# Stick-breaking attention: the reverse scan over the keys in pieces of 512 columns, right piece first

## The chip, the core and the metric

The kernel runs on one core of one Trainium2 chip. What counts is the device time of one execution in microseconds (us). Of the kernel before, three runs took 2499.8, 2501.02 and 2506.05 us; the median is 2501.02 us. The core has four engines that compute, each with its own queue of instructions in fixed order: TensorE (PE in the profile, with its weight loads listed apart as PEld), VectorE (DVE), ScalarE (ACT) and GpSimd (POOL). SyncE (SP) issues the transfers.

## What is computed

One layer of a hybrid decoder block on 1024 tokens of width 1024: a mixing sub-layer (stick-breaking attention with 16 heads of width 64, a state-space mixer and two gates), cross-attention into 256 memory tokens, and a dense SwiGLU layer. The change lies in the stick-breaking attention (the short description of the change calls it cross attention and speaks of maxima; the lines that it edits are those of this attention, and the scan is a running product with a floor). Cut to what matters:

```python
for blk in range(seq // SB_BLOCK):              # 8 blocks of 128 queries
    t0, t1 = blk * SB_BLOCK, (blk + 1) * SB_BLOCK
    z = jnp.einsum('bhtd,bhsd->bhts', qf[:, :, t0:t1], kf[:, :, :t1])
    causal = jnp.arange(t1)[None, :] < (t0 + jnp.arange(SB_BLOCK))[:, None]
    log_1mb = jnp.where(causal, jax.nn.log_sigmoid(-z), 0.0)
    tail = lax.cumsum(log_1mb, axis=3, reverse=True)
    w = jnp.where(causal, jnp.exp(z + tail), 0.0)
    outs.append(jnp.einsum('bhts,bhsd->bhtd', w, vf[:, :, :t1]))
```

With n = sigmoid(-z), the sum of logarithms becomes a running product of n from the right end of a row of keys to its left end. The weight of a key is the difference of two neighbouring products, and the kernel moves that difference over to the values, which it holds ready as differences of neighbouring rows (`dv_d`).

## The kernel before

**A head.** The 1024 queries of a head are eight blocks (b = 0 to 7) of 128. Block b sees the first (b + 1) x 128 keys. Blocks 0 to 3 are half 0, blocks 4 to 7 are half 1. `scores` works on one block: for each piece of up to 512 keys it issues two matmuls (L935, L936, tile `sc`; the second adds the low parts of the keys, `kl`) and a sigmoid on ScalarE (L937) into the tile `n`. When the whole row is there, one VectorE instruction (L939) runs over it from right to left in place: state = max(state x n, mask), from 1.0. The mask is 1 on and right of the diagonal and 0 elsewhere, so that the state stays 1 until the first visible key and is then the product. Block 4 thus has one scan of 640 columns, block 5 of 768, block 6 of 896 and block 7 of 1024.

**The values.** `values` works on one half. Step i takes the 128 keys of chunk i: `tr(i)` transposes those columns of each of the half's blocks on TensorE into one PSUM bank (L953, tile `tr`, two banks in turn); ScalarE takes 1 off and rounds to the high part (L956, `wth`); VectorE makes the low part (L957, `wtl`), which frees the bank. `av(i - 3)`, three steps behind, multiplies both parts with the values (L965, L966, tile `av`, one bank); ScalarE empties that bank at the end of a half (L969, `oT`). Chunk 0 comes first, and chunk 0 is the left end of each row, which the scan writes last.

**What surrounds them.** Each half's values are interleaved with the scores of the next half and with the q and k projections of a later pair of heads (L126 to L128, tile `mm`), as filler on TensorE. The projection's results go through ScalarE and VectorE (L891 to L902, tile `gt`) and then by transfer into `kh`, `kl` and `qs` (L884). VectorE also splits the projection's weights (L123, `wlo`).

**What sets the order.** The code gives every engine its work in the order of these interleaved lists, and a scheduler that goes by a simulated timeline then moves instructions of an engine past each other where no dependency forbids it. One tie is written by hand: the scan of block 6 (the seventh) is issued behind `lows[h, 0, 2]`, which is the `wtl` of chunk 2 in half 0 of the same head.

Of the kernel before, what the change touches and what calls it, by code (L numbers as in the profile page):

```python
# [12 lines left out]
ALU = mybir.AluOpType  # L13
# [4 lines left out]
S = 1024  # L18
# [3 lines left out]
HALF = 512  # L22
# [32 lines left out]
def hybrid_block(ctx, tc, a, out, dbg=None):  # L55
    nc = tc.nc
    V, A, T = [InTurn(tc, e) for e in (nc.vector, nc.scalar, nc.tensor)]
# [12 lines left out]
    def mk(pl, shape, dt, tag, bufs=None):  # L70
        uid[0] += 1
        kw = {} if bufs is None else {"bufs": bufs}
        return pl.tile(shape, dt, tag=tag, name=f"{tag}_{uid[0]}", **kw)
# [144 lines left out]
    def behind(marks):  # L218

        st = ExitStack()  # L220
        for m in marks:
            st.enter_context(tc.issue_after(m.ins))
        return st
# [52 lines left out]
    with ExitStack() as pa:  # L276
# [548 lines left out]
        with ExitStack() as p2:  # L825
# [13 lines left out]
            mask = mk(cb_, [P, S], BF16, "mask")  # L839
# [3 lines left out]
            marks, sig, highs, lows = [], [], [], {}  # L843
# [74 lines left out]
            def values_of(h):  # L918

                vt = heads[h]["v"] = mk(vp, [P, NCH, P], F32R, "v")  # L920
                nc.sync.dma_start(vt.bitcast(F32).rearrange("p c d -> p (c d)"), dv_d[h])

            def scores(h, half, tb, ns_):
                def run():
                    hd = heads[h]
                    if half == 0 and tb == 0:
                        values_of(h)
                    b = half * 4 + tb
                    L = (b + 1) * P
                    nt = mk(bp, [P, (half + 1) * HALF], F32, f"n{half}")  # L930
                    ns_.append(nt)
                    for s0 in range(0, L, HALF):
                        s1 = min(L, s0 + HALF)
                        ps = mk(psc, [P, HALF], F32, "sc")[:, :s1 - s0]
                        T.matmul(ps, hd["qs"][:, b * P:(b + 1) * P], hd["kh"][:, s0:s1], start=True, stop=False)  # L935
                        marks.append(T.matmul(ps, hd["qs"][:, b * P:(b + 1) * P], hd["kl"][:, s0:s1], start=False, stop=True))  # L936
                        sig.append(A.activation(nt[:, s0:s1], ps, AF.Sigmoid, scale=-(HD ** -0.5)))  # L937
                    with behind([lows[h, 0, 2]] if b == 6 else []):
                        V.tensor_tensor_scan(nt[:, 0:L][:, ::-1], nt[:, 0:L][:, ::-1], mask[:, S - L:][:, ::-1], 1.0, ALU.mult, ALU.max)  # L939
                return run  # L940

            LAG = 3
# [64 lines left out]
            for m in range(NM):  # L1007
                h, half = m // 2, m % 2
                hp, r = m // 4, m % 4
                s1 = [scores((m + 1) // 2, (m + 1) % 2, tb, ns_[m + 1]) for tb in range(4)] if m + 1 < NM else []  # L1010
# [1285 lines left out]
```

## Time and profile before

| what | before |
|---|---|
| median of three runs | 2501.02 us |
| the profiled execution, its own time | 2500.25 us |
| its span | 2498.5 us |
| TensorE busy over the span | 2438.4 us (98%) |
| VectorE, ScalarE, GpSimd busy | 1807.4 (72%), 1167.0 (47%), 604.5 us (24%) |
| L939, the scans: 128 of them | 170.0 us on VectorE |
| attention, 690 to 1000 us: TensorE, VectorE, ScalarE busy | 302.21, 233.66, 188.01 of 310 us |

The attention takes the stretch from about 660 to 1080 us of the span. One pair of heads repeats every 49.4 to 49.7 us in it. In a row of the timeline, the numbers are start and duration in us, then engine, line, operation, tile written and tile read, shape and count, and in brackets the idle time ahead of it on its engine with what ended it. Rows that belong together are merged ("x2"). Matmuls overlap: one of 512 columns lasts 0.39 us in the rows, and the next starts 0.23 us after it.

### The profile page before, as it was taken

To read this page: it belongs to the slowest core of one execution; us is meant where nothing else is said; L and a number is where in the kernel's file an instruction comes from. 1 tells how busy PE (TensorE), PEld (TensorE's weight loads), DVE (VectorE), ACT (ScalarE), POOL (GpSimd) and SP (SyncE) were. 2 spreads that over 40 slices of the span, in tenths; PEclk is the share of its full clock that TensorE was granted. 3 is DMA by queue.
4 is the path that set the end of the run, shared out by engine and by line. 5 is a ranking of instruction groups with operands and counts; after the bars stand their busy time and mean duration, and the time that the engine had idled before them with its cause. 6 is when DMAs were issued, how large, how long until landed. Compare 5 with 4: busy or idle time off the path is not lost. (4 is left out here: it accounts for less than half of the span.)

```text
span 2498.5 us, 33391 instructions
## 1 busy us (share of the span) xinstructions
PE 2438.4 (98%) x12306; PEld 2010.1 (80%) x12306; DVE 1807.4 (72%) x2261; ACT 1167.0 (47%) x2072; POOL 604.5 (24%) x505
## 2 busy tenths in 40 slices
PE   7999999999999999989999999999999999999998
PEld 5888788888788888877777778888888888888887
DVE  7767877767577777689888774577468556566997
ACT  5344455555465665566644312344335333344433
POOL 3221645443000000134444141102012322220001
PEclk9999999999999999999999999999999999999999
DMA  7565443333444334366332481321242322334322
GB/s 250 180 219 184 156 147 102 110 101 93 131 110 110 102 103 109 103 193 206 115 97 78 138 278 62 126 96 51 93 143 68 101 76 79 98 94 170 125 102 101
DMA packets 253741, 312.40 MB, mean 125 GB/s; under 512 B 17535, under 2 KB 169608, under 8 KB 253450
## 3 DMA queue, kind: packets, MB, share of 16 engines
q1 hardware_dynamic: 253290, 309.22, 38.8%
q8 instruction: 97, 1.59, 0.3%
q10 hardware_dynamic: 288, 1.05, 0.1%
q14 instruction: 66, 0.54, 0.1%
HBM read 210.59 MB, written 82.84 MB: 117 GB/s over the span
## 5 line engine op out<-in xcount | busy, mean ns | idle before, releaser
L939 DVE TENSOR_TENSOR_SCAN n<-n,mask 128x128 f32<-128x128 f32 (+7 forms) x128 | 170.0, 1350 | 27.7 <-ACT n L937 24.4
L123 DVE TENSOR_TENSOR sw<-sf,sw 128x512 fp32r<-128x512 f32 x142 | 127.0, 898 | 71.4 <-ACT sw L120 69.3
L120 ACT ACTIVATE sw<-sf 128x512 fp32r<-128x512 f32 x142 | 88.9, 628 | 157.4 <-PE mm L231 140.2
L956 ACT ACTIVATE wth<-tr,mone 128x512 fp32r<-128x512 f32 x192 | 110.7, 585 | 100.5 <-PE tr L953 100.1
L957 DVE SCALAR_TENSOR_TENSOR wtl<-tr,wth 128x512 fp32r<-128x512 f32 x192 | 101.8, 546 | 58.4 <-ACT wth L956 58.3
L732 DVE SCALAR_TENSOR_TENSOR b<-b,prmT,b 128x1023 f32<-128x1023 f32 (+2 forms) x72 | 110.5, 1534 | 16.9 <-ACT b L726 16.3
L123 DVE TENSOR_TENSOR sw<-wr,sw 128x512 fp32r<-128x512 f32 x107 | 98.8, 924 | 26.2 <-ACT sw L120 25.9
L230 PE MATMUL mm<-h,sw 128*128 128x512 f32 x288 | 112.0, 389 | 0.0
L231 PE MATMUL mm<-h,sw 128*128 128x512 f32 x288 | 111.7, 389 | 0.0
L116 POOL TENSOR_SCALAR whi<-wraw 128x1024 fp32r<-128x1024 f32 x13 | 14.8, 1136 | 395.0 <-PE mm L127 366.9
L229 PE MATMUL mm<-h,sw 128*128 128x512 f32 x288 | 109.9, 389 | 0.0
L197 POOL TENSOR_TENSOR sf<-wr,wr 128x512 f32<-128x512 f32 x36 | 53.1, 1476 | 228.8 <-DMA wr<-in_w_gu_dram 78.5
L126 PE MATMUL mm<-oth,bw 128*128 128x512 f32 x256 | 104.2, 407 | 4.2 <-DVE a L1289 2.6
L937 ACT ACTIVATE n<-sc 128x512 f32<-128x512 f32 (+1 forms) x192 | 86.7, 495 | 37.0 <-PE tr L953 20.6
L953 PE MATMUL tr<-ident,n 128*128 128x128 f32 x576 | 97.1, 275 | 6.1 <-DVE n L939 4.4
L128 PE MATMUL mm<-oth,bw 128*128 128x512 f32 x256 | 100.7, 393 | 0.0
L127 PE MATMUL mm<-otl,bw 128*128 128x512 f32 x256 | 100.6, 393 | 0.0
L128 PE MATMUL p<-bw,h 128*128 128x512 f32 x256 | 100.1, 392 | 0.5 <-DVE h L123 0.5
L174 POOL TENSOR_SCALAR rstd<-ms 128x1 f32<-128x1 f32 x74 | 28.0, 378 | 298.0 <-ACT x L181 226.8
L127 PE MATMUL p<-bw,h 128*128 128x512 f32 x256 | 99.9, 390 | 0.0
L126 PE MATMUL p<-bw,h 128*128 128x512 f32 x256 | 99.7, 390 | 0.0
L120 ACT ACTIVATE sw<-wr 128x512 fp32r<-128x512 f32 x107 | 67.1, 628 | 58.3 <-PE mm L231 51.4
(664 smaller groups left out, 7699.9 us busy)
## 6 DMA issues: line engine op xcount, KB each, us to landing
wr<-in_w_in_dram SPq DMA_DIRECT2D x36, 512.0 KB
wr<-in_w_gu_dram SPq DMA_DIRECT2D x72, 256.0 KB
zr<-in_w_in_dram SPq DMA_DIRECT2D x28, 512.0 KB
wraw<-in_w_in_dram SPq DMA_DIRECT2D x20, 512.0 KB
gu_d<-t SPq DMA_DIRECT2D x36, 256.0 KB
zs_d<-zo SPq DMA_DIRECT2D x32, 256.0 KB
dv_d<-v SPq DMA_DIRECT2D x16, 512.0 KB
xs_d<-b SPq DMA_DIRECT2D x32, 256.0 KB
```

The costliest lines, as they stand in the source:

```text
L120: A.activation(o, i, AF.Copy)
L123: return eng.tensor_tensor(o, i, hi.bitcast(F32), ALU.subtract)
L126: first = T.matmul(ps, sh, mh, start=start, stop=False)
L127: T.matmul(ps, sh, ml, start=False, stop=False)
L128: T.matmul(ps, sl, mh, start=False, stop=stop)
L229: T.matmul(ps, w[0][:, k, :], bh, start=first and k == 0, stop=False, skip_group_check=True)
L230: T.matmul(ps, w[0][:, k, :], bl, start=False, stop=False, skip_group_check=True)
L231: ins = T.matmul(ps, w[1][:, k, :], bh, start=False, stop=last and k == 3, skip_group_check=True)
L732: V.scalar_tensor_tensor(acc[:, sh:], y[:, :S - sh], cw(3 - sh, f), acc[:, sh:], ALU.mult, ALU.add)
L939: V.tensor_tensor_scan(nt[:, 0:L][:, ::-1], nt[:, 0:L][:, ::-1], mask[:, S - L:][:, ::-1], 1.0, ALU.mult, ALU.max)
L956: highs.append(A.activation(wh[:, t0 * P:], pt[:, t0 * P:], AF.Identity, bias=mone))
L957: lows[h, half, i] = V.scalar_tensor_tensor(wl[:, t0 * P:], pt[:, t0 * P:], -1.0, wh[:, t0 * P:].bitcast(F32), ALU.add, ALU.subtract)
```

## The change

The loop over the pieces of a row runs from right to left, so the matmuls and the sigmoid of the right piece come first. The scan moves into the loop: each piece of up to 512 columns is scanned by an instruction of its own as soon as its sigmoid is done. The right piece starts from 1.0, the left piece from the column at its right edge, nt[:, s1], which the scan ahead of it has written. Blocks 0 to 3 have one piece and are as before. Each of the blocks 4 to 7 has a right piece of 128, 256, 384 or 512 columns and a left piece of 512. Both pieces of block 6 keep the tie.

```diff
-                    for s0 in range(0, L, HALF):
+                    for s0 in range((L - 1) // HALF * HALF, -1, -HALF):
                         s1 = min(L, s0 + HALF)
                         ps = mk(psc, [P, HALF], F32, "sc")[:, :s1 - s0]
...
-                    with behind([lows[h, 0, 2]] if b == 6 else []):
-                        V.tensor_tensor_scan(nt[:, 0:L][:, ::-1], nt[:, 0:L][:, ::-1], mask[:, S - L:][:, ::-1], 1.0, ALU.mult, ALU.max)
+                        part = nt[:, s0:s1][:, ::-1]
+                        with behind([lows[h, 0, 2]] if b == 6 else []):
+                            V.tensor_tensor_scan(part, part, mask[:, S - L + s0:S - L + s1][:, ::-1], 1.0 if s1 == L else nt[:, s1:s1 + 1], ALU.mult, ALU.max)
```

The instructions are the same but for 64 more scans. Their order changes on TensorE, VectorE and ScalarE inside the attention, and at one place on SP, near its end, where three issues change places; after the attention nothing moves. The line numbers from L940 on are one higher in the changed kernel. The scan carries the name SCALAR_TENSOR_TENSOR in the listings of the order.

Place 1, VectorE, in the fifth head (in its timeline at 777.67 us). `n_1235` is the row of block 6, `n_1280` that of block 3 of the next head, `wtl_6815` (now `wtl_6835`) the low part of chunk 0 of half 1. Before:

```order
L957 SCALAR_TENSOR_TENSOR wtl_6740<-tr_6736,wth_6739 128x256
L939 SCALAR_TENSOR_TENSOR n_1235_6746<-n_1235_6746,mask_5385 128x896
L957 SCALAR_TENSOR_TENSOR wtl_6759<-tr_6756,wth_6758 128x128
L939 SCALAR_TENSOR_TENSOR n_1280_6914<-n_1280_6914,mask_5385 128x512
L957 SCALAR_TENSOR_TENSOR wtl_6815<-tr_6809,wth_6814 128x512
```

The same place in the changed kernel:

```order
L958 SCALAR_TENSOR_TENSOR wtl_6758<-tr_6754,wth_6757 128x256
L940 SCALAR_TENSOR_TENSOR n_1235_6764<-n_1235_6764,mask_5385 128x384
L958 SCALAR_TENSOR_TENSOR wtl_6778<-tr_6775,wth_6777 128x128
L940 SCALAR_TENSOR_TENSOR n_1280_6934<-n_1280_6934,mask_5385 128x512
L940 SCALAR_TENSOR_TENSOR n_1235_6764<-n_1235_6764,mask_5385 128x512
L958 SCALAR_TENSOR_TENSOR wtl_6835<-tr_6829,wth_6834 128x512
```

Block 6's left piece now stands behind `wtl` of chunk 3 and behind the scan of the next head's block 3, both of which stood behind block 6 before.

Place 2, TensorE, in the same head (timeline at 780.77 us), just after six matmuls L126 to L128. `tr_6809` (now `tr_6829`) is the bank of chunk 0 of half 1, `tr_6830` (now `tr_6850`) that of chunk 1; `n_1223`, `n_1229`, `n_1235`, `n_1242` are blocks 4, 5, 6 and 7. Blocks 4 and 5 of chunk 0 are transposed ahead of the six matmuls in both kernels. Before:

```order
L953 MATMUL tr_6809<-ident_89,n_1235_6746 128x128
L953 MATMUL tr_6809<-ident_89,n_1242_6771 128x128
L966 MATMUL av_6762<-wtl_6759,v_6552 128x128
L953 MATMUL tr_6830<-ident_89,n_1223_6702 128x128
L953 MATMUL tr_6830<-ident_89,n_1229_6723 128x128
L953 MATMUL tr_6830<-ident_89,n_1235_6746 128x128
L953 MATMUL tr_6830<-ident_89,n_1242_6771 128x128
L965 MATMUL av_6869<-wth_6814,v_6552 128x512
L953 MATMUL tr_6842<-ident_89,n_1223_6702 128x128
```

In the changed kernel:

```order
L967 MATMUL av_6781<-wtl_6778,v_6568 128x128
L954 MATMUL tr_6850<-ident_89,n_1223_6718 128x128
L954 MATMUL tr_6850<-ident_89,n_1229_6740 128x128
L954 MATMUL tr_6829<-ident_89,n_1235_6764 128x128
L954 MATMUL tr_6829<-ident_89,n_1242_6790 128x128
L954 MATMUL tr_6850<-ident_89,n_1235_6764 128x128
L954 MATMUL tr_6850<-ident_89,n_1242_6790 128x128
L966 MATMUL av_6889<-wth_6834,v_6568 128x512
L954 MATMUL tr_6862<-ident_89,n_1223_6718 128x128
```

The transposes of blocks 6 and 7 for chunk 0 moved behind half of chunk 1's, and everything of chunks 0 and 1 now ends directly ahead of the first `av` of the half. On ScalarE, `oT` of the half before moved ahead of chunk 0's `wth` there.

Place 3, TensorE, in the sixth head (timeline at 803.35 us). `n_1307` is block 6, `n_1314` block 7; `sc` with `kh` and `kl` are the scores of blocks 4 and 5 of the next half. Before, from the transposes of blocks 6 and 7 for chunk 0:

```order
L953 MATMUL tr_7079<-ident_89,n_1307_7015 128x128
L953 MATMUL tr_7079<-ident_89,n_1314_7040 128x128
L966 MATMUL av_7034<-wtl_7031,v_6822 128x128
L953 MATMUL tr_7102<-ident_89,n_1295_6974 128x128
L953 MATMUL tr_7102<-ident_89,n_1301_6995 128x128
L953 MATMUL tr_7102<-ident_89,n_1307_7015 128x128
L953 MATMUL tr_7102<-ident_89,n_1314_7040 128x128
L126 MATMUL mm_7111<-b21h_118,whi_7090 128x512
```

After that come five more matmuls of the projection, four of scores, and the first `av` of the half. In the changed kernel the six matmuls L126 to L128 and six of scores stand ahead of the transposes of blocks 6 and 7:

```order
L935 MATMUL sc_7269<-kh_6961,qs_6691 128x128
L935 MATMUL sc_7274<-kh_6961,qs_6691 128x512
L936 MATMUL sc_7274<-kl_6963,qs_6691 128x512
L935 MATMUL sc_7291<-kh_6961,qs_6691 128x256
L936 MATMUL sc_7269<-kl_6963,qs_6691 128x128
L936 MATMUL sc_7291<-kl_6963,qs_6691 128x256
L954 MATMUL tr_7103<-ident_89,n_1307_7037 128x128
L954 MATMUL tr_7103<-ident_89,n_1314_7063 128x128
L954 MATMUL tr_7126<-ident_89,n_1307_7037 128x128
L954 MATMUL tr_7126<-ident_89,n_1314_7063 128x128
L966 MATMUL av_7166<-wth_7108,v_6842 128x512
```

Further up at places 2 and 3, one pair of score matmuls of 512 columns has moved: at place 2 that of block 5's left piece, from ahead of the place to behind it, with 256 columns of its right piece taking its turn; at place 3 that of block 4's left piece, from some 1.5 us ahead of the place into the six of the list above.

## Prediction

> **What bounds the kernel now.** I read the page first, then the attention alone, since only its order moves, then what TensorE waits for in it, then the timelines of one even and one odd head.
>
> The page's span and the busy time of the engines over it:
>
> ```profile
> span 2498.5 us, 33391 instructions
> PE 2438.4 (98%) x12306; PEld 2010.1 (80%) x12306; DVE 1807.4 (72%) x2261; ACT 1167.0 (47%) x2072; POOL 604.5 (24%) x505
> ```
>
> The stretches of time, here 690 to 1010 us (length, then busy us of PE, PEld, DVE, ACT, POOL, then the granted clock):
>
> ```profile
> 690.00:1010.00 320.00, 311.65 (x1707) 260.34 (x1707) 241.63 (x297) 192.91 (x391) 7.36 (x7) 1.00 0.40 109
> ```
>
> TensorE is busy in 311.65 of 320 us at full clock, VectorE in 241.63. So TensorE bounds the attention, and VectorE matters only where TensorE stands still for it. The waits of the weight loads, which come just ahead of their matmuls, say where, over the same stretch:
>
> ```profile
> PEld tr L953 <- DVE n L939: 6.9, 7, 1.0
> PEld av L965 <- ACT oT L969: 5.9, 6, 1.0
> ...
> PEld av L966 <- DVE wtl L957: 1.3, 7, 0.2
> ...
> PEld sc L936 <- issue: 0.5, 1, 0.5
> ```
>
> Seven odd heads lose 0.98 us each to a scan, six even heads 0.98 us each to `oT`. Both lie where chunk 0 of half 1 begins. That is where the order moves, so what is asked is how long TensorE stands there afterwards.
>
> **The work added.** Groups of the scans by shape on VectorE (total, mean ns of one):
>
> ```profile
> L939 DVE TENSOR_TENSOR_SCAN n<-n,mask 128x896 f32<-128x896 f32 x16 | 32.2, 2013 | 0.0
> L939 DVE TENSOR_TENSOR_SCAN n<-n,mask 128x640 f32<-128x640 f32 x16 | 23.8, 1490 | 5.5 <-ACT n L937 2.2 <-PE av L965 2.0
> L939 DVE TENSOR_TENSOR_SCAN n<-n,mask 128x512 f32<-128x512 f32 x16 | 19.4, 1211 | 1.4 <-ACT n L937 1.4
> L939 DVE TENSOR_TENSOR_SCAN n<-n,mask 128x384 f32<-128x384 f32 x16 | 14.9, 932 | 0.0
> L939 DVE TENSOR_TENSOR_SCAN n<-n,mask 128x128 f32<-128x128 f32 x16 | 6.4, 400 | 1.4 <-ACT n L937 1.4
> ```
>
> Block 6 becomes 0.932 + 1.211 = 2.143 for 2.013 us, +0.13; block 4 0.400 + 1.211 for 1.490, +0.12. With 0.13 for each of the 64 divided rows it is 8.3 us of VectorE. The Trainium skill, "Perfetto Trace Analysis", section "Optimizing Scalar/DVE Operations", puts some 60 ns of access overhead on each VectorE instruction on SBUF, by which 64 more would be 3.8 us, less than half of what the rows give. Either sum lies on an engine that is idle for 78 of these 320 us. I cost it at nothing except in block 6, where TensorE waits for the row. Were this cover gone, the whole 8.3 us would be paid. The sigmoids and score matmuls are the same in number, and cost nothing by count.
>
> The left piece reads a column that the right one writes, so VectorE waits for itself. No row shows such a pair of scans. The nearest rows are those of VectorE below, where independent neighbours start 0.07 to 0.08 us before the one ahead ends (779.91 + 0.26 = 780.17 against 780.10; 777.98 + 2.01 = 779.99 against 779.91). A pair in order loses at least nothing and at most that and as much again, some 0.15 us; a gain has no mechanism. In block 6 another instruction stands between the pieces, so I take the overlap alone, 0.05 to 0.08, as lost there, and nothing in the others, whose first reader comes later.
>
> **An even head (the fifth).** VectorE's timeline, before:
>
> ```profile
> 774.48 1.23 DVE L123 TENSOR_TENSOR wlo<-wraw,whi 128x1024 fp32r<-128x1024 f32 x1 [0.65 <-ACT whi L120]
> ...
> 776.22 1.53 DVE L939 TENSOR_TENSOR_SCAN n<-n,mask 128x256 f32<-128x256 f32 x2
> ...
> 777.98 2.01 DVE L939 TENSOR_TENSOR_SCAN n<-n,mask 128x896 f32<-128x896 f32 x1
> 779.91 0.26 DVE L957 SCALAR_TENSOR_TENSOR wtl<-tr,wth 128x128 fp32r<-128x128 f32 x1
> 780.10 1.21 DVE L939 TENSOR_TENSOR_SCAN n<-n,mask 128x512 f32<-128x512 f32 x1
> 781.91 0.69 DVE L957 SCALAR_TENSOR_TENSOR wtl<-tr,wth 128x512 fp32r<-128x512 f32 x1 [0.60 <-ACT wth L956]
> ```
>
> From 774.48 to 781.31 VectorE has no idle time, so its order alone decides when block 6 is ready: at 779.99. TensorE and ScalarE there:
>
> ```profile
> 780.77 0.38 PE L953 MATMUL tr<-ident,n 128*128 128x128 f32 x2
> 780.91 0.31 PE L966 MATMUL av<-wtl,v 128*128 128x128 f32 x1
> 781.05 0.62 PE L953 MATMUL tr<-ident,n 128*128 128x128 f32 x4
> 782.42 0.50 PE L965 MATMUL av<-wth,v 128*128 128x512 f32 x1 [0.74 <-ACT oT L969]
> 782.75 0.60 PE L953 MATMUL tr<-ident,n 128*128 128x128 f32 x4
> 781.19 0.69 ACT L956 ACTIVATE wth<-tr,mone 128x512 fp32r<-128x512 f32 x1 [3.75 <-PE tr L953]
> ```
>
> Block 6 was 0.8 us early. In the new order (place 1) the right piece runs 777.98 to 778.91, `wtl` to about 779.1, the next head's block 3 to 780.23, and the left piece to 780.23 + 1.21 = 781.44. TensorE comes to it at about 780.77 - 0.23 + 0.28 = 780.82: 512 columns of scores became 256 ahead of it (a pair of 512 is 0.46, one of 256 0.23), and one `av` and two transposes came in. It waits 0.6 us until T = 781.44.
>
> Then the chain of chunk 0 runs: from the transposes to `wth` 781.19 - 780.77 = 0.42, to `wtl` 0.72, its length 0.69, and 0.14 until the matmul behind it (rows below: 801.92 + 0.40 = 802.32, matmul at 802.46), together 1.97. Before, TensorE had the scores of chunk 1 and a wait for `oT` to lie over it. Now `oT` is early (its hold of 0.98 goes), but the banks of chunks 0 and 1 are both full, and `tr` of chunk 2 is late next: 781.44 + 1.97 = 783.41 against 782.75, +0.66. The 0.23 of scores not yet done is repaid a few us later, and nothing behind 782.75 waits. So **+0.89 a head, six of them: +5.3.**
>
> **An odd head (the sixth).** VectorE, TensorE and its weight load:
>
> ```profile
> 801.92 0.40 DVE L957 SCALAR_TENSOR_TENSOR wtl<-tr,wth 128x256 fp32r<-128x256 f32 x1
> 802.24 2.02 DVE L939 TENSOR_TENSOR_SCAN n<-n,mask 128x896 f32<-128x896 f32 x1
> 802.37 0.19 PEld L966 LDWEIGHTS av<-wtl,v 128*128 128x128 f32 x1 [0.19 <-DVE wtl L957]
> 802.46 0.30 PE L966 MATMUL av<-wtl,v 128*128 128x256 f32 x1
> 803.35 0.39 PE L128 MATMUL mm<-b11h,wlo 128*128 128x512 f32 x1
> 804.31 0.44 PE L953 MATMUL tr<-ident,n 128*128 128x128 f32 x2 [0.57 <-DVE n L939]
> 806.49 0.51 PE L935 MATMUL sc<-kh,qs 128*128 128x128 f32 x2
> 806.84 0.45 PE L936 MATMUL sc<-kl,qs 128*128 128x512 f32 x2
> 807.13 0.44 PE L965 MATMUL av<-wth,v 128*128 128x512 f32 x1
> 807.41 0.60 PE L953 MATMUL tr<-ident,n 128*128 128x128 f32 x4
> ```
>
> The new order moves one 512-column pair from ahead of the `av` at 802.46 to behind it. TensorE already waits there for `wtl`, whose place on VectorE is unchanged, so the 0.46 us bring nothing early. From 803.58 (803.35 + 0.23) come one `av` and two transposes (0.31), six matmuls (1.46) and six of scores (0.64 for those four, from 806.49 to 807.13, and 0.24 for the 256-column pair): 806.2. The left piece ends at about 802.24 + 0.93 + 0.2 + 1.21 + 1.21 = 805.8, so the hold of 0.98 on the scan goes. But again the chain of 1.97 follows with little to lie over it: `tr` of chunk 2 at 808.17 against 807.41, +0.76, and 0.23 of scores owed: **+1.0 a head, seven of them: +7.0.**
>
> **The keys' low part.** The changed order reaches the scores with the new `kl` sooner. Its transfer and the one wait for it that the stretch holds, in two odd heads:
>
> ```profile
> 801.36 2.51 SPq L884 DMA_DIRECT2D kl<-gt  x4
> ```
>
> ```profile
> 751.46 2.52 SPq L884 DMA_DIRECT2D kl<-gt  x4
> 757.59 0.19 PEld L936 LDWEIGHTS sc<-kl,qs 128*128 128x128 f32 x1 [0.46 <-issue]
> ```
>
> Before, TensorE comes to it about 5.7 us behind the first issue and once found it missing until 6.1; now at about 806.0, 4.6 behind. Landing by 4.6 costs nothing, landing at 5.7 costs 1.1 a head, 7.7 in all. The single miss in seven says that the landings lie well inside 5.7, so I take 0.3 a head: **+2.**
>
> **The last head.** It has no following scores:
>
> ```profile
> 1065.80 2.47 DVE L1081 SCALAR_TENSOR_TENSOR wraw<-wraw,rstd,wraw 128x1024 f32<-128x1024 f32 x2
> 1068.93 0.66 PE L953 MATMUL tr<-ident,n 128*128 128x128 f32 x4 [0.97 <-DVE wtl L957]
> ```
>
> On VectorE one of these two (1.24 us) now stands ahead of block 6's right piece and one between its pieces. The left piece then ends near 1068.3, and chunk 2 starts near 1070.25: **+1.3.** SP's three moved issues lie near the end, and I cost them at nothing, since no wait of TensorE there is for a transfer.
>
> Sum: 5.3 + 7.0 + 2 + 1.3 = 15.6. The profiled execution took 2500.25 us, 0.8 under the median of 2501.02; 2500.25 + 15.6 = 2515.9, **2516 us**. The runs lie within 2499.8 to 2506.05, so 0.3% (7.5 us, to 2493.5 and 2508.5) is about what a measurement can tell from no change.
>
> **Rivals.** *An even trade.* The holds only change place: 0.98 per head go, and the hold on chunk 0's `wtl` comes, 1.97 less what lies over it, four transposes (about 0.34, from 781.05) and the first `av` (0.33, 782.42 to 782.75), so 1.3. It holds if the left piece is ready when TensorE comes (even heads) and the moved scores don't lie idle (odd heads): 13 x 0.3 gives 2504. For it: VectorE's 78 idle us. Against it: no idle time in the rows from 774.48 to 781.31.
>
> *Faster, the other side.* Earlier pieces take away the scan's hold: 7 x 0.98 = 6.9 us, 2493.4. This decides if block 6's left piece ends before TensorE's arrival (780.82 in the even head) and chunk 0's chain still lies beside other matmuls. The odd head speaks for the first half, the order of place 2 and 3 against the second, since both banks fill together. The Trainium skill, "Perfetto Trace Analysis", section "Optimizing Scalar/DVE Operations", speaks for this: "If Scalar/Vector aren't saturated, but are causing bubbles on other engines, breaking up instructions may allow work to be completed sooner." By that rule the seven holds of 6.9 us, which the waits do show, would go.
>
> *The transfer decides.* `kl` lands late in all odd heads, 1.1 instead of 0.3: 15.6 - 2 + 7.7 gives 2521.6. The one miss speaks for it, its being one of seven against it.
>
> *No effect.* The first reader of a row reads its left end, which is written last in both kernels; a right piece done early frees nothing by itself. That is no separate time: without the new order it would be the 2501 us of before, and I count it with the even trade.
>
> **How the numbers follow.** The forecast has 0.60, the even trade 0.20, the faster case 0.08, the late transfer 0.12. The forecast alone runs from 2505 to 2521 (transfer at nothing and two thirds off both head terms; or the transfer at its upper end), with 0.10 of its 0.60 below 2508.5. Slower: 0.50 + 0.12 = 0.62. Same: 0.20 + 0.10 + 0.03 of the faster case that falls short = 0.33. Faster: 0.05. The range, 2500 to 2523, leaves out the faster case, and a tenth in all beyond its ends.
>
> **What would show it.** 64 more scans, of 1.21 us on the left: 8 us more of VectorE. The waits of `tr` for the scan gone in odd heads and some 0.6 us long in even heads; those of `av` for `oT` gone; a new wait of `tr` or `av` for `wtl` or `wth` of chunk 0, over 1 us in each head; waits of `sc` for `kl` in the odd ones. A pair of heads would take 2 us more than the 49.4 to 49.7 of before. I am wrong if VectorE reaches block 6's left piece earlier than its order of before suggests, or if the chain from the transposes to `wtl` runs shorter than 1.97 us.

## The result, and the profile after

The changed kernel takes 2515.59 us (median, 2514.01 to 2516.98). The kernel before, run beside it, takes 2502.97 us (2499.8 to 2506.05). The ratio is 1.0055, with a 95% interval of 1.0043 to 1.0067: some 12.6 us slower. The forecast was 2516 us, slower.

The page of the changed kernel, its span and engine totals:

```profile
span 2513.4 us, 33487 instructions
PE 2446.0 (97%) x12306; PEld 2011.6 (80%) x12306; DVE 1810.6 (72%) x2325; ACT 1168.5 (46%) x2072; POOL 600.0 (24%) x505
```

The span has grown by 14.9 us, from 2498.5. The instructions are the same but for the 64 scans, and the attention, which the heads pass through later and later, holds all of the difference. `oT` of head 0, half 0, starts 0.15 us later than before, that of the last head's half 1 14.82 us later (the timelines of ScalarE). The stretch 690 to 1010 us of the changed kernel:

```profile
690.00:1010.00 320.00, 306.28 (x1648) 252.28 (x1648) 238.89 (x337) 188.65 (x380) 6.31 (x6) 1.00 0.38 103
```

TensorE's busy time has fallen from 311.65 to 306.28 of 320 us at full clock: it stands still more. The waits of its weight loads (total us, times, longest), over 690 to 1017 us, so that the seventh odd head's wait for chunk 2's `wtl` is in it as before (its chunk 0 comes later, at 1019.82):

```profile
PEld av L966 <- ACT wth L957: 9.6, 12, 0.8
PEld tr L954 <- DVE wtl L958: 7.6, 18, 0.5
PEld av L967 <- DVE wtl L958: 4.3, 7, 0.6
PEld tr L954 <- DVE n L940: 4.3, 6, 0.7
PEld sc L936 <- DMA kl<-gt: 0.4, 1, 0.4
PEld sc L935 <- DMA kh<-kh: 0.3, 1, 0.3
PEld sc L936 <- issue: 0.2, 1, 0.2
```

The holds of before, 0.98 on the scan in odd heads and 0.98 on `oT` in even heads, are gone. In their place each of the twelve heads whose chunk 0 lies in this stretch is held 0.80 us for its `wth` and 0.54 for its `wtl`; even heads also wait 0.72 for block 6's left piece, odd heads 0.62 for chunk 2's `wtl` (0.19 before).

An even head (the fifth), VectorE's and then TensorE's timeline:

```profile
782.03 0.95 DVE L940 TENSOR_TENSOR_SCAN n<-n,mask 128x384 f32<-128x384 f32 x1
782.89 0.26 DVE L958 SCALAR_TENSOR_TENSOR wtl<-tr,wth 128x128 fp32r<-128x128 f32 x1
783.08 2.39 DVE L940 TENSOR_TENSOR_SCAN n<-n,mask 128x512 f32<-128x512 f32 x2
786.72 1.29 DVE L958 SCALAR_TENSOR_TENSOR wtl<-tr,wth 128x512 fp32r<-128x512 f32 x2 [1.25 <-ACT wth L957]
```

```profile
784.65 0.39 PE L954 MATMUL tr<-ident,n 128*128 128x128 f32 x2
785.52 0.66 PE L954 MATMUL tr<-ident,n 128*128 128x128 f32 x4 [0.49 <-DVE n L940]
786.74 0.49 PE L966 MATMUL av<-wth,v 128*128 128x512 f32 x1 [0.56 <-ACT wth L957]
787.46 0.66 PE L954 MATMUL tr<-ident,n 128*128 128x128 f32 x4 [0.23 <-DVE wtl L958]
```

The left piece is the second of the two scans merged at 783.08; it ends at 785.47, and the transposes start at 785.52. From there to the transposes of chunk 2 at 787.46 are 1.94 us, which hold four transposes and one `av`. The odd head that follows has the same chain, without the wait for the left piece. The last row is VectorE's, with the left piece second:

```profile
807.23 0.39 PE L967 MATMUL av<-wtl,v 128*128 128x256 f32 x1 [0.21 <-DVE wtl L958]
...
811.05 0.60 PE L954 MATMUL tr<-ident,n 128*128 128x128 f32 x4
812.21 0.49 PE L966 MATMUL av<-wth,v 128*128 128x512 f32 x1 [0.56 <-ACT wth L957]
812.93 0.66 PE L954 MATMUL tr<-ident,n 128*128 128x128 f32 x4 [0.23 <-DVE wtl L958]
...
808.14 2.39 DVE L940 TENSOR_TENSOR_SCAN n<-n,mask 128x512 f32<-128x512 f32 x2
```

VectorE's work, the scans by shape over the attention:

```profile
L940 DVE TENSOR_TENSOR_SCAN n<-n,mask 128x512 f32<-128x512 f32 x96 | 119.9, 1261 | 11.7 <-ACT n L937 9.8
L940 DVE TENSOR_TENSOR_SCAN n<-n,mask 128x384 f32<-128x384 f32 x32 | 30.1, 940 | 0.0
L940 DVE TENSOR_TENSOR_SCAN n<-n,mask 128x256 f32<-128x256 f32 x32 | 21.8, 680 | 0.0
L940 DVE TENSOR_TENSOR_SCAN n<-n,mask 128x128 f32<-128x128 f32 x32 | 13.1, 409 | 4.7 <-ACT n L937 4.6
```

Together 184.9 us. The eight shapes of before sum to 172.9 in the same view, so the pieces add 12.0 us, 0.19 a further scan.

### The profile page after: what moved, and what is told of

The parts are those of the page before. It is cut to its first block, busy times and chain, and to the rows that moved or that the text cites. A ratio compares the mean times of both kernels' runs of the same rounds, so it can differ in the third digit from the quotient of the medians.

```text
span 2513.4 us, 33487 instructions
## 1 busy us (share of the span) xinstructions
PE 2446.0 (97%) x12306; PEld 2011.6 (80%) x12306; DVE 1810.6 (72%) x2325; ACT 1168.5 (46%) x2072; POOL 600.0 (24%) x505
## 5 line engine op out<-in xcount | busy, mean ns | idle before, releaser
L940 DVE TENSOR_TENSOR_SCAN n<-n,mask 128x128 f32<-128x128 f32 (+3 forms) x192 | 181.0, 969 | 16.4 <-ACT n L937 14.4
L126 PE MATMUL mm<-oth,bw 128*128 128x512 f32 x256 | 104.6, 409 | 4.7 <-DVE a L1290 2.6
L937 ACT ACTIVATE n<-sc 128x128 f32<-128x128 f32 (+2 forms) x192 | 86.7, 494 | 39.4 <-PE tr L954 22.1
L128 PE MATMUL mm<-oth,bw 128*128 128x512 f32 x256 | 100.9, 394 | 0.0
L128 PE MATMUL p<-bw,h 128*128 128x512 f32 x256 | 100.1, 392 | 0.5 <-DVE h L123 0.5
L126 PE MATMUL p<-bw,h 128*128 128x512 f32 x256 | 99.8, 390 | 0.0
```

What stands on the lines that cost most here:

```text
L126: first = T.matmul(ps, sh, mh, start=start, stop=False)
L128: T.matmul(ps, sl, mh, start=False, stop=stop)
L940: V.tensor_tensor_scan(part, part, mask[:, S - L + s0:S - L + s1][:, ::-1], 1.0 if s1 == L else nt[:, s1:s1 + 1], ALU.mult, ALU.max)
```

## The experiments

The theory: what costs is not the pieces' work but where block 6's left piece, and with it the transposes of chunks 0 and 1, ends up in the planned order. Rival A: the order of the scores. Rival B: the 64 further scans and their waits for each other, which at 0.2 us each would be 12.8 us, as large as the measured loss. All differences below are against the kernel before on the same chip; us are the ratio's excess of 2501 (for the change 13.8, where the two medians differ by 12.6).

| experiment | further scans | ratio (95%) | us |
|---|---|---|---|
| the change | 64 | 1.0055 (1.0043 to 1.0067) | +13.8 |
| right piece's scores first, one scan | 0 | 1.0019 (1.0011 to 1.0028) | +4.8 |
| left first, two scans | 64 | 1.0042 (1.0030 to 1.0055) | +10.5 |
| block 6 unchanged | 48 | 1.0007 (0.9998 to 1.0016) | +1.8 |
| only block 6 changed | 16 | 1.0052 (1.0039 to 1.0064) | +13.0 |
| no dependency between the pieces | 64 | 1.0031 (1.0020 to 1.0042) | +7.8 |
| left piece ahead of block 3 | 64 | 1.0030 (1.0021 to 1.0040) | +7.5 |
| right piece of block 6 not tied | 64 | 1.0002 (0.9993 to 1.0011) | +0.5 |
| pieces, no tie | 64 | 1.0032 (1.0020 to 1.0045) | +8.0 |
| one scan, no tie | 0 | 1.0000 (0.9991 to 1.0009) | 0 |
| one scan, block 6 ahead of blocks 1 and 2 | 0 | 1.0000 (0.9992 to 1.0009) | 0 |
| middle chunks first, pieces | 64 | 1.0072 (1.0060 to 1.0085) | +18.0 |
| middle chunks first, one scan | 0 | 1.0137 (1.0123 to 1.0151) | +34.3 |

**The parts alone.** The scores' order by itself:

```diff
-                    for s0 in range(0, L, HALF):
+                    for s0 in range((L - 1) // HALF * HALF, -1, -HALF):
```

> Only the order of the score pieces is changed (right piece first); each row has its one scan as before. Theory (the loss is the uncovered chain of chunk 0, banks of chunks 0 and 1 filling together, which follows from the two-piece scan of block 6): around chunk 0 the order stays as before, so no hold for wth/wtl of chunk 0. What stays of the loss is the 512-column pair that in odd heads moved behind the hold for wtl (0.46 us idle ahead of it): 7 x 0.46 = 3.2 us, 0.1%. Rival A (the order of the scores makes the loss): about the whole 12.6 us. Rival B (the work and own waits of 64 more scans make it, 0.2 us each): 0 us.

Measured +4.8 (2.8 to 7.0). Rival A falls: the order of the scores alone makes about a third of the loss, half of it at the upper end of the interval. Its waits show the part that the theory gives it, `av` held for chunk 2's `wtl` 4.4 us in seven odd heads, where before it was 1.3; the holds on the scan and on `oT` are those of before.

Two scans alone, the scores as before:

```diff
-                    with behind([lows[h, 0, 2]] if b == 6 else []):
-                        V.tensor_tensor_scan(nt[:, 0:L][:, ::-1], nt[:, 0:L][:, ::-1], mask[:, S - L:][:, ::-1], 1.0, ALU.mult, ALU.max)
+                    for s0 in range((L - 1) // HALF * HALF, -1, -HALF):
+                        s1 = min(L, s0 + HALF)
+                        part = nt[:, s0:s1][:, ::-1]
+                        with behind([lows[h, 0, 2]] if b == 6 else []):
+                            V.tensor_tensor_scan(part, part, mask[:, S - L + s0:S - L + s1][:, ::-1], 1.0 if s1 == L else nt[:, s1:s1 + 1], ALU.mult, ALU.max)
```

> Scores left piece first as before; each row of blocks 4 to 7 is scanned by two instructions once both sigmoids stand. Theory: the order at chunk 0 is the changed kernel's (transposes of blocks 6 and 7 for chunks 0 and 1 together), so even heads lose 0.66 and odd ones 0.55 (no scores owed now): 6 x 0.66 + 7 x 0.55 = 7.8, with 1.1 each at the first and last heads 10 us. Rival A (scores' order): about 0. Rival B (64 more scans): 12.6 us.

Measured +10.5, between the theory's 10 and rival B's 12.6, so it tells only against A.

**Work or place.** The next two take the scans apart by block: the pieces (right first) for `b != 6` alone, and for `b == 6` alone (this one is shown); the other blocks keep the loop and the scan of before.

```diff
+                    for s0 in (range((L - 1) // HALF * HALF, -1, -HALF) if b == 6 else range(0, L, HALF)):
...
+                        if not (b == 6):
+                            continue
+                        part = nt[:, s0:s1][:, ::-1]
...
```

> Blocks 4, 5 and 7 as in the changed kernel (right piece first, two scans), block 6 as before (one scan, left piece first): 48 of the 64 further scans stay. Theory: chunk 0's order is that of before, so its holds are too; the moved scores of odd heads remain, 7 x 0.46: 3 us over before. Rival B (each further scan costs 0.2 us): 9.5 us. Rival A (scores' order): 10 us or more.

> Only block 6 as in the changed kernel, blocks 4, 5 and 7 as before: 16 of the 64 further scans. Theory: the holds on chunk 0's wth (0.80) and wtl (0.54) stand in every head from the second on, 10 us over before as with two scans everywhere. Rival B (0.2 us a scan): 3 us. Rival A: 3 us or less, since one block in four has its scores reordered.

48 further scans cost 1.8 us (-0.5 to 4.0), the 16 of block 6 cost 13.0 (9.8 to 16.0). By rival B it would be 9.5 and 3. So the pieces' work is not the loss; the division of block 6 is. The waits of the second, with block 6 alone in pieces (690 to 1010 us, as in all that follow):

```profile
PEld av L971 <- ACT wth L962: 9.6, 12, 0.8
PEld tr L959 <- DVE wtl L963: 6.5, 12, 0.5
PEld tr L959 <- DVE n L942: 3.3, 6, 0.6
```

These are the changed kernel's: 12 times 0.80 for `wth` of chunk 0, 12 times 0.54 for `wtl`. In the same stretch it waits 3.1 us for the keys (`kh`, `kl`, issue), where before there was 0.5. Whether this is what it has above the expected 10 stays open: the profiled execution, at 2518.65 us, lies 4.5 above the median of its kernel.

**The tie on the right piece.** The tie belonged to one scan. In the change it binds both pieces behind chunk 2's `wtl`, though the left one follows the right one anyway. With the tie on the left piece alone:

```diff
-                        with behind([lows[h, 0, 2]] if b == 6 else []):
+                        with behind([lows[h, 0, 2]] if b == 6 and s1 < L else []):
```

> The changed kernel with the tie on the left piece of block 6 alone; its right piece is free. All 64 further scans stay. Theory: the planner runs the right piece far earlier, the left piece then comes 1.21 us behind wtl of chunk 2, some 0.8 us sooner than block 6's whole scan did, and TensorE's order at chunk 0 is that of before. Odd heads lose 0.46 to the moved scores and save up to 0.73 of the hold on the scan; even heads keep the hold for oT: between 2 us under and 3 us over before. Rival B (64 more scans, 0.2 us each): 12 us over.

Measured 1.0002 (-1.8 to 2.8 us): the time of before, with all 64 scans, the reordered scores and the dependent pieces in place. Its waits, and its scans of 512 columns:

```profile
PEld av L967 <- DVE wtl L958: 7.1, 13, 0.6
PEld av L966 <- ACT oT L970: 5.9, 6, 1.0
PEld tr L954 <- DVE n L940: 1.7, 7, 0.2
```

```profile
L940 DVE TENSOR_TENSOR_SCAN n<-n,mask 128x512 f32<-128x512 f32 x96 | 120.4, 1255 | 10.4 <-ACT n L937 8.6
```

The scans cost VectorE as much as in the changed kernel (120.4 against 119.9 us), yet chunk 0's holds are gone. The hold on the scan has fallen from 6.9 to 1.7 us, as an earlier block 6 should have it, and holds for `wtl` have grown from 1.3 to 7.1. This shows that the loss of the change needs the tied right piece. That the further scans cost nothing here holds in sum only. By the starts of `oT`, an odd head (fourth to twelfth) is now 0.25 to 0.51 us faster than before and an even head (third to eleventh) 0.42 to 0.48 slower: chunk 6's `wtl` of the half that ends there stands behind the freed right piece (two scans together, 2.12 us from 744.11), and holds `av` for 0.48.

**The late left piece, and the chain behind it.** One tie more in the changed kernel puts the left piece ahead of the next head's block 3:

```diff
-                        with behind([lows[h, 0, 2]] if b == 6 else []):
+                        with behind([lows[h, 0, 2]] if b == 6 else [left6[h - 1]] if b == 3 and h else []):
...
```

Here `left6[h]` is the last scan of block 6 in head `h`.

> The changed kernel with one more tie: the scan of block 3 of the next head stands behind block 6's left piece. TensorE's order stays the changed kernel's. Theory: the left piece is ready 1.21 us sooner, so the hold of tr on the scan in the six even heads (0.72) goes, but the uncovered chain of chunk 0 (0.80 for wth, 0.54 for wtl) stays in all: 6 x 0.6 = 3.6 us less than the changed kernel, 9 us over before. If the late left piece made the whole loss: at most 3 us over before.

Measured +7.5 (5.3 to 10.0) against the change's +13.8. TensorE's wait for the scan is gone from the list; the chain of chunk 0 and the hold of the moved scores are left:

```profile
PEld av L967 <- ACT wth L958: 7.7, 11, 0.8
PEld tr L955 <- DVE wtl L959: 7.5, 18, 0.5
PEld av L968 <- DVE wtl L959: 4.3, 7, 0.6
```

The gain of some 6 us is more than the 3.6 expected: besides the 4.3 us on the scan, the holds for `wth` fell from 9.6 to 7.7. What each part is worth shows in the starts of `oT`. An even head (third to thirteenth) loses 0.14 to 0.21 us here against before, where it lost 0.81 to 0.87 in the change. An odd head loses 0.44 to 0.74 here (the last one 1.66), and the moved scores alone, in the first experiment, make 0.21 to 0.49 of it. So the late left piece is the largest part of the loss, and the moved scores come next. The chain, though its holds are the longest in the list, costs only some 0.2 us a head beyond the 0.98 that it replaces (an estimate from these starts).

**The dependency.** With 1.0 in place of `nt[:, s1:s1 + 1]` (the running product is then not carried over the edge):

> The changed kernel, but each left piece starts from 1.0 instead of the column that the right piece wrote (the running product isn't carried over the edge, which leaves that dependency out): all 64 further scans stay. Theory: the planner now puts both pieces of block 6 next to each other and leaves chunk 0's transposes where they were before, so the holds are those of before; block 6 is 0.13 us later, which the odd heads pay, and their moved scores leave 0.46 idle: 7 x 0.6 = 4 us over before. Rival B (64 more scans cost 0.2 us each, whatever their order): 12 us. Rival B' (it is the own wait on the chip, at 64 pairs): 0 us.

Measured +7.8 (5.0 to 10.5), more than the 4 expected and less than rival B's 12. The holds are those of before (6.2 on the scan, 5.9 on `oT`), with 3.9 for chunk 2's `wtl` and 2.8 that the expectation had not counted, for `kh`: its order puts the next scores ahead of six projection matmuls, and TensorE comes to them before the transfer has landed. That the planner leaves chunk 0 alone when the dependency is gone is shown; that its own wait costs nothing on the chip is not, since the order differs. On VectorE itself it does have a price (last section).

**No tie at all.** The pieces, and the kernel before, each with `behind([])`:

> The changed kernel without any tie on block 6. Theory: both pieces run early, all eight transposes of chunks 0 to 1 stand apart with six projection matmuls between, so neither the hold on the scan nor the uncovered chain is there; 0.46 in odd heads for the moved scores stays: 5 us under to 3 us over before. If the tie keeps something else early (TensorE waits for wtl of chunks 2 and 3 behind the early scans): over before by more. Rival B: 12 us over.

> The kernel before without the tie on block 6: the same early place for block 6 with one scan a row. Theory: the hold on the scan in odd heads (7 x 0.98) and for oT in even ones (6 x 0.98) can go: up to 12 us under before; if VectorE's early scans hold up wtl or the projection's gt instead, no gain. Against the kernel of pieces without a tie it gives the price of the pieces alone: 3 us by the theory, 12 us by rival B.

Without pieces: 0, where up to 12 us of gain were possible. With pieces: +8.0 (5.0 to 11.3), above the expected range. In neither is there a hold on the scan, and both pay elsewhere, in `av` for a `wtl`, the longest once in each pair of heads: that of chunk 6 in the half that ends there, which VectorE now reaches behind the next head's scans of blocks 5 and 6. VectorE at such a place, first with one scan a row, then with pieces (with TensorE's hold in the last row):

```profile
743.87 3.66 DVE L939 TENSOR_TENSOR_SCAN n<-n,mask 128x768 f32<-128x768 f32 x2
747.45 0.60 DVE L957 SCALAR_TENSOR_TENSOR wtl<-tr,wth 128x256 fp32r<-128x256 f32 x2
```

```profile
743.24 3.51 DVE L940 TENSOR_TENSOR_SCAN n<-n,mask 128x512 f32<-128x512 f32 x3
746.67 0.59 DVE L958 SCALAR_TENSOR_TENSOR wtl<-tr,wth 128x256 fp32r<-128x256 f32 x2
747.12 0.19 PEld L967 LDWEIGHTS av<-wtl,v 128*128 128x128 f32 x1 [1.89 <-DVE wtl L958]
```

Block 6 early means some 3.5 us of scans ahead of that `wtl`, which the tie keeps apart. In all, `av` waits 9.6 us for `wtl` with one scan and 16.3 with pieces. Against each other the two kernels were to give the price of the pieces alone: 3 us by the theory, 12 by rival B. The 8.0 lies between, and bears out neither. The reordered scores, which alone cost 4.8 (2.8 to 7.0), are among it, so how much of it is the scans stays open. "The pieces are free" holds only for the orders in which they are covered.

**Two attempts at a faster kernel.** In the first, the kernel before ties the scans of blocks 1 and 2 of the next head behind block 6:

```diff
-                    with behind([lows[h, 0, 2]] if b == 6 else []):
+                    with behind([lows[h, 0, 2]] if b == 6 else [six[h - 1]] if b in (1, 2) and h else []):
...
```

> The kernel before with one more tie: the scans of blocks 1 and 2 of the next head stand behind block 6's, which so begins 1.5 us sooner. TensorE's order at chunk 0 stays. Theory (the hold on the scan in odd heads is block 6's place on VectorE): that hold goes, 0.73 of PE time, and with it most of the hold of av for wtl of chunk 2 ahead of it, 7 x 0.85 = 6 us under before, 2495; even heads keep theirs. If the hold comes back at blocks 1 and 2 of the next head: no gain.

No gain (-2.0 to 2.3 us). The hold on the scan is gone, and the next instruction takes it over:

```profile
753.92 3.44 DVE L940 TENSOR_TENSOR_SCAN n<-n,mask 128x896 f32<-128x896 f32 x3
757.29 0.26 DVE L958 SCALAR_TENSOR_TENSOR wtl<-tr,wth 128x128 fp32r<-128x128 f32 x1
```

```profile
757.60 0.33 PE L967 MATMUL av<-wtl,v 128*128 128x128 f32 x1 [0.53 <-DVE wtl L958]
```

The chain on VectorE is as long as before, and now its last member, chunk 3's `wtl`, holds TensorE 0.53 us, where the scan had held it 0.57. In the second attempt the chunks of half 1 come in the order 4 to 7, 0 to 3, so that the first transposes read right pieces only:

```diff
+                seq = [4, 5, 6, 7, 0, 1, 2, 3] if half else [0, 1, 2, 3]
...
-                            tr(i)
+                            tr(seq[i])
...
```

> The changed kernel, and the values of half 1 take the chunks in the order 4, 5, 6, 7, 0, 1, 2, 3. Chunks 4 to 7 lie in the right pieces, so the first transposes need no left piece. Theory (the first reader decides): the holds on the scan, on oT and for wtl around the half's begin go (0.98 and 0.19 in odd heads, 0.98 in even ones), 7 x 1.17 + 6 x 0.98 = 14 us under before, 2487; with half of it taken by new holds 2494. Rival B (work of 64 more scans): the changed kernel's time or more.

> The kernel before (scores left piece first, one scan a row), with the chunks of half 1 in the order 4, 5, 6, 7, 0, 1, 2, 3. Theory: chunk 4 needs the whole row, as chunk 0 did, so the holds on the scan stay to a part; the order of transposes, spread between scores and projections, covers chunk 4's chain: between 2490 and before's 2501. If it is as fast as with two scans, the order of the chunks is worth it all and the pieces nothing.

Both expectations fell: +18.0 and +34.3. With the pieces the hold on the scan did vanish, and larger ones came:

```profile
PEld tr L956 <- DVE wtl L960: 13.4, 19, 1.1
PEld mm L126 <- DVE gt L902: 9.2, 6, 1.5
PEld av L968 <- ACT wth L959: 6.6, 13, 0.6
```

With one scan a row:

```profile
PEld tr L955 <- DVE wtl L959: 16.7, 17, 2.1
PEld sc L935 <- DMA kh<-kh: 12.1, 6, 3.3
...
PEld tr L955 <- DVE n L939: 2.2, 6, 0.4
```

Where the chunks go this way, the kernel with pieces (and with the reordered scores) is 16 us faster (18.0 against 34.3). The right piece then has a reader that needs nothing else, but that is not shown to be the reason: the hold on the scan that went is 2.2 us, and the larger difference is the wait for `kh`. Which of the new waits is cause and which is consequence stays open. No version ran faster than the kernel before.

## Why the prediction was right, point by point

**The bound.** TensorE's standing still decided, as said: its number of matmuls is the same, its waits are not.

**Even heads, +0.89 each, 5.3.** The starts of `oT` put the six (the third to the thirteenth) at 0.81 to 0.87, together 5.1. The left piece behind block 3, the wait on it (forecast 0.6; 0.49 of PE time, 0.72 by its weight loads), and the 1.97 from there to chunk 2 (measured 1.94) were all found. The fifth head starts 4.05 us late (`oT` of the head before); with that taken off, its left piece ends at 781.42 (forecast 781.44) and chunk 2 starts at 783.41 (forecast 783.41). With the left piece moved ahead of block 3, +0.86 shrinks to some 0.2, so this term was right in its mechanism too.

**Odd heads, +1.0 each, 7.0, and +2 for `kl`.** Together 7.5 against 9. Four of the seven have 0.75 to 0.91; three have 1.19, 1.30 and 1.55, and these are the ones that wait for transfers. That wait exists, in three heads rather than a little in all, some 1.4 us in sum, and part of it is for `kh`, which the forecast did not name. In the sixth head, 4.85 us late, TensorE comes to the transposes at 806.20 (forecast 806.2), the left piece is done at 805.68 (805.8), and chunk 2 starts at 808.08 (808.17).

**The first head** was left out, and lost 1.0: `oT` is 0.15 later in its half 0 and 1.14 in its half 1. VectorE there, then the row of TensorE, in the changed kernel:

```profile
679.86 4.15 DVE L940 TENSOR_TENSOR_SCAN n<-n,mask 128x512 f32<-128x512 f32 x5
683.92 1.26 DVE L958 SCALAR_TENSOR_TENSOR wtl<-tr,wth 128x512 fp32r<-128x512 f32 x2
684.65 0.66 PE L954 MATMUL tr<-ident,n 128*128 128x128 f32 x4 [0.64 <-DVE wtl L958]
```

Five scans stand ahead of chunk 0's `wtl`, which before began at 682.88.

**The last head, +1.3.** The last two heads together lost 1.1.

**The sum** was 15.6; the trace has 14.8, of which the forecast's own terms make 13.7 and the first head the rest: the odd heads were 1.5 too dear, and the missing head 1.0 too cheap. The errors nearly cancel, so the 0.4 us by which 2516 missed the median is luck. The sum was put on a single execution of 2500.25 us, and the median of before came out at 2502.97: the profiled execution itself lies 14.9 above that of before, the medians 12.6.

**VectorE's work, +8.3 at no cost.** Its size was too small: 12.0 by the durations, or 0.19 a scan. What was missed is that a piece which starts from a column lasts longer, and that two pieces in order take 0.27 us more than two independent ones, where 0.15 was put as the most (both in the last section). The comparison with the 60 ns of the Trainium skill, "Perfetto Trace Analysis", section "Optimizing Scalar/DVE Operations", was a misreading: that section calls them engine-busy time and puts the profiled latency at about twice as much. The trace agrees: of the 0.13 in the durations, 0.08 is overlap with the neighbour, and 0.05 is left. That this work costs nothing is shown in sum for the order with the right piece untied, and for blocks 4, 5 and 7 within -0.5 to 4.0 us; without any tie it isn't.

**The rivals.** The even trade came close in one respect: the holds did change place, but the new ones are longer (0.80 + 0.54 against 0.98, and the moved scores and the left piece on top). The rule quoted from the Trainium skill, "Perfetto Trace Analysis", section "Optimizing Scalar/DVE Operations", is not borne out by the change: the holds on the scan in odd heads do go, but not because the row is done sooner. In the sixth head block 6 was done at 804.26 before, and its left piece at 805.68, with the 4.85 us taken off; TensorE only comes later. The instructions that were broken up were given other places. With the right piece untied the rule holds for the scan itself: the holds on the scan fell by 5.2 us, holds for `wtl` grew by 5.8, and nothing was gained.

## What to carry to other kernels

When an instruction with a hand-written tie is divided, ask of each part whether the tie is still meant for it: here a tie on the wrong half cost 13 us, and with the tie on the other half alone the same 64 instructions cost nothing measurable in sum. Cost a divided instruction by the order that it brings about, above all by when its last part now runs and what still lies over the chain behind it, and not by its own duration. And when a hold on one instruction is removed, look who is next in the same queue: three edits that removed the hold on the scan or most of it gained nothing, and in each a `wtl` on VectorE held TensorE longer than before.

## What was not expected of the hardware

A scan that starts from a column which another scan has written takes longer than one that starts from a constant. In the changed kernel the 64 left pieces last 1.26 to 1.29 us each (one lasts 2.00), and the 32 scans of 512 columns that start from 1.0 last 1.19 to 1.23. In the kernel without the dependency, where all 96 start from 1.0, none is longer than 1.24:

```profile
L940 DVE TENSOR_TENSOR_SCAN n<-n,mask 128x512 f32<-128x512 f32 x96 | 114.7, 1208 | 10.2 <-ACT n L937 10.0
```

A left piece that stands directly behind its right piece also begins later. The two scans of block 4, in the changed kernel and then in the one without the dependency:

```profile
792.53 1.80 DVE L940 TENSOR_TENSOR_SCAN n<-n,mask 128x128 f32<-128x128 f32 x2
792.31 1.53 DVE L940 TENSOR_TENSOR_SCAN n<-n,mask 128x128 f32<-128x128 f32 x2
```

One scan of 640 columns took 1.49 us before. So dividing a row costs 0.04 us of VectorE's time by itself, and 0.31 with the dependency, where nothing stands between the pieces.
